# Inside each product of the feed-forward pairs: rounded weights first, the remainder's passes behind them

## Chip, core and metric

One core of a Trainium2 chip runs the whole kernel. The metric is the device time of one execution in microseconds (us); the time of a kernel is the median of several runs. Five engines matter here: TensorE (PE, with its weight loads shown apart as PEld), VectorE (DVE), ScalarE (ACT), GpSimd (POOL, which here mostly issues DMAs that add one tile to another) and SyncE (SP, which issues the loads).

## The reference, cut to what matters

The block is a state-space and short-convolution mixer followed by a gated feed-forward part; 512 positions, model width 2048, feed-forward width 5632. The change is in the first product of the feed-forward part, `xn @ w_up`:

```python
def conv_ffn(xn, w_up, ffn_conv_w, ffn_conv_b, w_down):
    h = xn @ w_up                                       # (512, 2048) @ (2048, 11264)
    a = causal_dwconv(h[..., :D_FF], ffn_conv_w, ffn_conv_b)
    return (jax.nn.gelu(a) * h[..., D_FF:]) @ w_down
```

Everything is float32. The result must be that of float32 products.

## The kernel before

**Three passes for one product.** TensorE is fed with the type fp32r. A weight tile W is split on the chip into a rounded part hi (ACT, line 152, tile `whi`) and the remainder lo = W - hi (DVE, line 131, tile `wlo`), and the activations likewise into xh and xl. A 128x128 block of a product is then three passes of TensorE that add into the same PSUM tile: hi on xh, hi on xl, lo on xh. Each pass is one weight load (PEld) and one matmul (PE); the hi block is loaded twice, once for xh and once for xl.

**Chunks.** All weight tiles of the kernel stand in one list, `flat`; an entry is 128 partitions by up to 1024 elements, that is up to 8 blocks (j = 0 to 7). `whi` and `wlo` have three buffers each. The passes of an entry are emitted first, and then, in `after` or `after_pair`, what ACT and DVE do for the entries that follow: `prep_to(i + 3)` emits the rounding and the remainder of the entry two places on. The order on each engine is the order in which the Python code emits it; nothing reorders it later.

**The feed-forward pairs.** For each of 44 blocks of feed-forward channels both halves of `w_up` are needed, each over 2048 inputs: four weight tiles of 1024 by 128. The first block is done plainly (units `ua` and `ub`, 512 columns of moving data per pass, `products` outside the class). The other 43 are the class `Pair` (G = 1 to 43): sums and differences of the four tiles are multiplied with sums and differences of the activations of the two sequence halves (LO and HI, 256 columns each), so that seven products replace eight. A pair has seven entries, here called products c = 0 to 6, each of 8 blocks and so of 24 passes over 256 columns. Lines 1041, 1042 and 1043 are the three passes: hi on xh, hi on xl, lo on xh. Moving data are `x2h`/`x2l`, `th`/`tl` and, for c = 6, the tile `xga`. The PSUM tiles are called `sr`.

**What runs around a product.** After product c, `after_pair` emits `sums(c)` (reads of finished PSUM tiles: ACT lines 1050 and 1059, DVE lines 1053 to 1063), the rounding for the entry two places on, the remainders that are due (`lo_all`), and `rest(c)`: sums of raw weights for the next pair (DVE lines 995 and 1007, ACT copy line 1001, and POOL's adding DMAs, lines 996 and 1008), loads of the pair after that (SP, line 984), and the steps of the gate of the previous pair (convolution on DVE, lines 1072 and 1075, and the gelu on ACT, line 1076). So, in a steady pair, ACT has the gelu of the previous pair (emitted after product 1) ahead of the rounding for product 4 (emitted after product 2), and that gelu waits for a convolution step on DVE.

**Where the other order is already in use.** `products` for all other units (lines 164 to 173) first runs through hi on xh and hi on xl for all blocks and then through lo on xh. Those have 512 columns, but for the last eight units of the kernel (`ends`), which have 256.

Of the kernel before, what the change touches and what calls it, by code (L numbers as in the profile page):

```python
# [16 lines left out]
P = 128  # L17
# [50 lines left out]
def block_kernel(ctx: ExitStack, tc: tile.TileContext, a: dict):  # L68
    nc = tc.nc
# [88 lines left out]
    def products(i, j0, j1):  # L158

        u, c = flat[i]  # L160
        if u.ps is None:
            u.ps = psm.tile([P, T], F32, tag="mm", name="mm")
        base = sum(x[1] for x in u.chunks[:c])
        hi, lo = preps[i]
        for j in range(j0, j1):
            xh, xl = (x[:, u.cols] for x in u.xs(base + j))
            w = slice(j * P, (j + 1) * P)
            nc.tensor.matmul(u.ps[:, u.cols], hi[:, w], xh, start=base + j == 0, stop=False)  # L168
            nc.tensor.matmul(u.ps[:, u.cols], hi[:, w], xl, start=False, stop=False)  # L169
        for j in range(j0, j1):  # L170
            xh = u.xs(base + j)[0][:, u.cols]
            nc.tensor.matmul(u.ps[:, u.cols], lo[:, j * P:(j + 1) * P], xh, start=False,  # L172
                             stop=base + j == u.total - 1)
# [35 lines left out]
    def run(i0, i1):  # L209
        for i in range(i0, i1):  # L210
            u, c = flat[i]
            if u.chunks[c][0] is None:
                u.products(i, c)
                after_pair(i)
                continue
            if c == 0 and u.pre:
                u.pre()
            products(i, 0, u.chunks[c][1])
            after(i)
# [454 lines left out]
    for i in range(3, 19):  # L674
        u, c = flat[i]
        u.hooks.setdefault(c, []).append(lambda: next(params))

    def start():
# [40 lines left out]
        for z in zpad:  # L719
            nc.vector.memset(z[:, 0:2], 0.0)  # L720
        products(0, 0, 6)
        products(1, 0, 6)
        products(0, 6, 8)
        preps.pop(0)
# [285 lines left out]
    class Pair:  # L1010
# [21 lines left out]
        def products(self, i, c):  # L1032
            hi, lo = preps[i]
            name = ("p1", "px", "p6", "py", "p1", "px", "py")[c]
            if c < 4:
                self.ps[name] = ff["pss"].tile([P, T], F32, tag="sr", name="sr")[:, 0:T // 2]
            ps = self.ps[name]
            for j in range(8):
                xh, xl = self.moving(c, j)
                w = slice(j * P, (j + 1) * P)  # L1040
                nc.tensor.matmul(ps, hi[:, w], xh, start=(c < 4 and j == 0), stop=False, skip_group_check=c >= 4)  # L1041
                nc.tensor.matmul(ps, hi[:, w], xl, start=False, stop=False, skip_group_check=c >= 4)  # L1042
                nc.tensor.matmul(ps, lo[:, w], xh, start=False, stop=j == 7, skip_group_check=c >= 4)  # L1043


        def sums(self, c):
# [250 lines left out]
```

## Time and profile before

| | |
|---|---|
| median of 3 runs | 2515.23 us (2514.97 to 2516.53) |
| the profiled execution | 2517.59 us, its span 2515.6 us |
| granted TensorE clock, mean | 0.997 |
| busy: PE / PEld / DVE / ACT / POOL | 2482.3 / 2184.4 / 1665.4 / 1079.2 / 565.4 us |
| pairs on PE: first matmul to start of the last | 1166.5 to 2017.5 us of the span |

A PE that is "busy" in a profile is not a PE at its peak: a matmul is shown from its start to its modelled end (0.28 us here), while the next one starts 0.11 to 0.12 us after it. What passes cost is therefore read from the distance between starts, and waits from the idle time before weight loads.

### The profile page before, as it was taken

How to read it: one execution, taken by the hardware profiler on the slowest of the kernel's cores; microseconds unless marked ns; L12 is line 12 of the kernel's file. 1: busy time of each engine (PE TensorE's matmuls, PEld its weight loads, DVE VectorE, ACT ScalarE, POOL GpSimd, SP SyncE). 2: the span in 40 equal slices, each digit the busy share in tenths (PEclk: the TensorE clock that was granted, in tenths of full speed). 3: DMA queues.
4: the chain of work that ended last, by engine and by line, in shares of the span. 5: the costliest groups of instructions: out<-in, count | busy, mean ns of one | idle time of the engine just before them, and what ended most of it. 6: DMA issues, size and time to landing. Idle time of an engine off the chain costs nothing.

```text
span 2515.6 us, 36421 instructions
## 1 busy us (share of the span) xinstructions
PE 2482.3 (99%) x14616; PEld 2184.4 (87%) x14616; DVE 1665.4 (66%) x1924; ACT 1079.2 (43%) x1384; POOL 565.4 (22%) x424
## 2 busy tenths in 40 slices
PE   8999999999999999999999999999999999999997
PEld 6888888777888888888999999999999988888887
DVE  7799889999224464447777777887777753333334
ACT  5355444553234333335455544555454432222233
POOL 1077777778003121110000000000000000000011
PEclk9999999999999999999999999999999999999998
DMA  5777777786345344444666666666666663434335
GB/s 180 228 191 189 186 189 202 192 208 185 132 167 184 109 142 139 151 138 144 174 174 167 170 184 180 184 177 176 182 181 175 197 243 115 129 112 128 97 93 160
DMA packets 149209, 418.40 MB, mean 166 GB/s; under 512 B 17712, under 2 KB 26032, under 8 KB 149040
## 3 DMA queue, kind: packets, MB, share of 16 engines
q1 hardware_dynamic: 121584, 330.88, 41.4%
q0 software_dynamic: 20448, 74.46, 15.8%
q10 hardware_dynamic: 7008, 10.74, 1.2%
q8 instruction: 114, 1.87, 0.3%
q14 instruction: 55, 0.45, 0.1%
HBM read 300.67 MB, written 40.89 MB: 136 GB/s over the span
## 4 chain that ended last, share of the span: by engine, by line
PE 84%; DVE 7%; DMA 4%; issue 3%; ACT 2%; SPq 0%; DVEq 0%; ACTq 0%; POOLq 0%
PE mm L168 19%; PE mm L169 19%; PE mm L172 19%; PE sr L1043 8%; PE sr L1042 8%; PE sr L1041 8%; DVE wlo L131 2%; DMA wraw<-wraw 2%; ACT whi L152 2%; DVE zz L487 1%; DVE wraw L995 1%; DVE ph L452 0%; PE w L476 0%; DMA braw<-in_b 0%; DMA xgb<-xgb 0%
## 5 line engine op out<-in xcount | busy, mean ns | idle before, releaser
L131 DVE TENSOR_TENSOR wlo<-wraw,whi 128x1024 fp32r<-128x1024 f32 (+1 forms) x396 | 486.0, 1228 | 325.7 <-ACT whi L152 287.1
L152 ACT ACTIVATE whi<-wraw 128x1024 fp32r<-128x1024 f32 (+1 forms) x396 | 393.9, 998 | 382.3 <-PE mm L169 332.6
L168 PE MATMUL mm<-xh,whi 128*128 128x512 f32 x1344 | 527.6, 393 | 10.6 <-ACT whi L103 5.8
L169 PE MATMUL mm<-xl,whi 128*128 128x512 f32 x1344 | 526.0, 391 | 0.0
L1043 PE MATMUL sr<-x2h,wlo 128*128 128x256 f32 x1376 | 386.5, 281 | 2.9 <-DVE wlo L131 1.6
L1041 PE MATMUL sr<-x2h,whi 128*128 128x256 f32 x1376 | 383.4, 279 | 0.8 <-ACT whi L152 0.8
L1042 PE MATMUL sr<-x2l,whi 128*128 128x256 f32 x1376 | 383.3, 279 | 0.0
L172 PE MATMUL mm<-xh,wlo 128*128 128x512 f32 x1344 | 332.9, 389 | 2.4 <-DMA wlo<-wraw 2.4
L168 PEld LDWEIGHTS mm<-xh,whi 128*128 128x128 f32 x1344 | 253.5, 189 | 72.2 <-ACT whi L103 5.8
L172 PEld LDWEIGHTS mm<-xh,wlo 128*128 128x128 f32 x1344 | 252.1, 188 | 56.4 <-DMA wlo<-wraw 4.1
L169 PEld LDWEIGHTS mm<-xl,whi 128*128 128x128 f32 x1344 | 253.5, 189 | 54.3 <-DVE xl L108 1.8
L1043 PEld LDWEIGHTS sr<-x2h,wlo 128*128 128x128 f32 x1376 | 258.9, 188 | 6.9 <-DVE wlo L131 6.5
L1041 PEld LDWEIGHTS sr<-x2h,whi 128*128 128x128 f32 x1376 | 259.0, 188 | 1.1 <-ACT whi L152 1.0
L1042 PEld LDWEIGHTS sr<-x2l,whi 128*128 128x128 f32 x1376 | 259.7, 189 | 0.0
L1043 PE MATMUL sr<-th,wlo 128*128 128x256 f32 x688 | 192.2, 279 | 1.3 <-DVE wlo L131 1.3
L1042 PE MATMUL sr<-tl,whi 128*128 128x256 f32 x688 | 192.0, 279 | 0.0
L168 PE MATMUL mm<-x2h,whi 128*128 128x512 f32 (+1 forms) x528 | 191.9, 371 | 0.0
L1041 PE MATMUL sr<-th,whi 128*128 128x256 f32 x688 | 191.9, 279 | 0.0
L169 PE MATMUL mm<-x2l,whi 128*128 128x512 f32 (+1 forms) x528 | 191.2, 369 | 0.0
L875 POOL TENSOR_TENSOR acc<-acc,sq 128x512 f32<-128x512 f32 (+1 forms) x31 | 38.8, 1250 | 641.9 <-ACT sq L873 641.9
L131 DVE TENSOR_TENSOR wlo<-r,whi 128x1024 fp32r<-128x1024 f32 x88 | 107.5, 1222 | 49.2 <-ACT whi L152 49.2
L1008 POOL DMA_DIRECT2D wraw<-wraw x43 | 37.0, 861 | 446.8 <-DVE ap L1061 422.2
(253 smaller groups left out, 4593.2 us busy)
## 6 DMA issues: line engine op xcount, KB each, us to landing
wraw<-in_w_in SPq DMA_DIRECT2D x127, 512.0 KB, 4.3
r<-in_w_up SPq DMA_DIRECT2D x88, 512.0 KB, 5.9
xgb<-in_w_up SPq DMA_DIRECT2D x84, 512.0 KB, 5.3
wraw<-in_w_down SPq DMA_DIRECT2D x104, 384.0 KB, 3.2
wlo<-wraw POOLq DMA_DIRECT2D x56, 512.0 KB, 5.4
wraw<-wraw POOLq DMA_DIRECT2D x43, 512.0 KB, 9.6
wraw<-in_w_o SPq DMA_DIRECT2D x32, 512.0 KB, 3.6
r<-r POOLq DMA_DIRECT2D x22, 512.0 KB, 4.6
```

Source lines behind the costliest of these rows:

```text
L131: nc.vector.tensor_tensor(o, x, y, op=ALU.subtract)
L152: nc.scalar.activation(hi[:, w], raw[:, w], AF.Copy)
L168: nc.tensor.matmul(u.ps[:, u.cols], hi[:, w], xh, start=base + j == 0, stop=False)
L169: nc.tensor.matmul(u.ps[:, u.cols], hi[:, w], xl, start=False, stop=False)
L172: nc.tensor.matmul(u.ps[:, u.cols], lo[:, j * P:(j + 1) * P], xh, start=False, stop=base + j == u.total - 1)
L487: nc.vector.tensor_tensor(z, z, t, op=ALU.subtract if j else ALU.add)
L875: nc.gpsimd.tensor_tensor(acc[:, cols], acc[:, cols], ff["sq"][:, cols], op=ALU.add)
L995: nc.vector.tensor_tensor(s, r[:, 2], r[:, 3], op=ALU.add)
L1008: nc.gpsimd.dma_start(gs[G]["s4"], s, accum_op=ALU.add)
L1041: nc.tensor.matmul(ps, hi[:, w], xh, start=(c < 4 and j == 0), stop=False, skip_group_check=c >= 4)
L1042: nc.tensor.matmul(ps, hi[:, w], xl, start=False, stop=False, skip_group_check=c >= 4)
L1043: nc.tensor.matmul(ps, lo[:, w], xh, start=False, stop=j == 7, skip_group_check=c >= 4)
```

## The change

Within one product of a pair the order of the 24 passes changes. Before, each block j had its three passes together. Now the 16 passes with hi (two for each block) come first and the 8 with lo behind them. Nothing else is touched: the passes, their operands, the PSUM tile and what all other engines are given stay as they are.

```diff
                 w = slice(j * P, (j + 1) * P)
                 nc.tensor.matmul(ps, hi[:, w], xh, start=(c < 4 and j == 0), stop=False, skip_group_check=c >= 4)
                 nc.tensor.matmul(ps, hi[:, w], xl, start=False, stop=False, skip_group_check=c >= 4)
-                nc.tensor.matmul(ps, lo[:, w], xh, start=False, stop=j == 7, skip_group_check=c >= 4)
+            for j in range(8):
+                nc.tensor.matmul(ps, lo[:, j * P:(j + 1) * P], self.moving(c, j)[0], start=False, stop=j == 7,
+                                 skip_group_check=c >= 4)
```

On PE, at the beginning of the first product of pair 1, the program before has these rows (line, operation, output<-moving,weights; in brackets the semaphores waited for: those of ACT for the rounded weights, those of DVE for the remainder):

```order
L1041 MATMUL sr<-x2h,whi 128x256 [waits Activation_49]
L1042 MATMUL sr<-x2l,whi 128x256
L1043 MATMUL sr<-x2h,wlo 128x256 [waits DVE_49]
L1041 MATMUL sr<-x2h,whi 128x256
L1042 MATMUL sr<-x2l,whi 128x256
L1043 MATMUL sr<-x2h,wlo 128x256
```

The end of the same product in the changed program, and the start of the next one (a row with x7 stands for seven alike):

```order
L1041 MATMUL sr<-x2h,whi 128x256
L1042 MATMUL sr<-x2l,whi 128x256
L1041 MATMUL sr<-x2h,whi 128x256
L1042 MATMUL sr<-x2l,whi 128x256
L1044 MATMUL sr<-x2h,wlo 128x256 [waits DVE_49]
L1044 MATMUL sr<-x2h,wlo 128x256 x7
L1041 MATMUL sr<-th,whi 128x256 [waits Activation_49]
```

The wait for the remainder has moved from the third pass of a product to its seventeenth; the wait for the rounded weights stays on the first. Line 1043 of before is line 1044 in the changed kernel.

On ACT, in pair 2 of the program before, these rows run from the rounding for product 3 to the copy of product 4's PSUM tile:

```order
L152 ACTIVATE whi<-r 128x1024 [waits DMASW4_49,Activation_49]
L1076 ACTIVATE cv<-cv 128x512 [waits DVE_49]
L152 ACTIVATE whi<-r 128x1024 [waits PE_49,Activation_49]
L152 ACTIVATE whi<-wraw 128x1024 [waits DMASW5_49,PE_49,Activation_49]
L1001 ACTIVATE wraw<-xgb 128x1024 [waits DMAHW2_49]
L1059 ACTIVATE ap<-sr 128x256 [waits PE_49]
```

In the changed program the same place reads:

```order
L152 ACTIVATE whi<-r 128x1024 [waits DMASW4_49,Activation_49]
L1078 ACTIVATE cv<-cv 128x512 [waits DVE_49]
L152 ACTIVATE whi<-r 128x1024 [waits PE_49,Activation_49]
L152 ACTIVATE whi<-wraw 128x1024 [waits DMASW5_49,PE_49,Activation_49]
L1001 ACTIVATE wraw<-xgb 128x1024 [waits DMAHW2_49]
L1061 ACTIVATE ap<-sr 128x256 [waits PE_49]
```

Only line numbers differ (1076 is 1078, 1059 is 1061): ACT, and DVE likewise, keep their order. The second row is the gelu, the third the rounding for product 4, behind it.

## Rows read from the trace of the kernel before

**Rows 1.** The page, part 1: busy us (share of span) xinstructions.

```profile
PE 2482.3 (99%) x14616; PEld 2184.4 (87%) x14616; DVE 1665.4 (66%) x1924; ACT 1079.2 (43%) x1384; POOL 565.4 (22%) x424
```

**Rows 2.** Lines 1043 and 1041: ns min/median/max, first and last start, forms.

```profile
L1043 PE MATMUL sr<-xga,wlo x344: 276/281/388, 1185.5 to 2017.5; 128*128 128x256 f32 x172
...
L1041 PE MATMUL sr<-x2h,whi x1376: 276/280/387, 1166.5 to 2014.5; 128*128 128x256 f32 x197
```

**Rows 3.** Who waited for whom: us in total, times, longest us.

```profile
PEld sr L1043 <- DVE wlo L131: 9.7, 25, 1.5
```

**Rows 4.** PE timeline (start us, us), pair 4: first and last of 105 consecutive matmuls.

```profile
1229.73 0.28 PE L1042 MATMUL sr<-xga,whi 128*128 128x256 f32 x1
...
1241.97 0.28 PE L1041 MATMUL sr<-x2h,whi 128*128 128x256 f32 x1
```

**Rows 5.** PE timeline, pairs 26 and 27: first and last of 108 consecutive matmuls.

```profile
1681.78 0.28 PE L1042 MATMUL sr<-xga,whi 128*128 128x256 f32 x1
...
1693.92 0.28 PE L1041 MATMUL sr<-x2h,whi 128*128 128x256 f32 x1
```

**Rows 6.** Groups on PE, 1167:1172, 1230:1242, 1682:1694 us: busy us, mean ns.

```profile
L1041 PE MATMUL sr<-th,whi 128*128 128x256 f32 x8 | 2.2, 281 | 0.0
...
L1041 PE MATMUL sr<-x2h,whi 128*128 128x256 f32 x17 | 4.8, 281 | 0.0
...
L1043 PE MATMUL sr<-th,wlo 128*128 128x256 f32 x16 | 4.4, 276 | 0.0
```

**Rows 7.** Stretches: us, then PE, PEld, DVE, ACT, POOL busy (x), PEclk, DMA share, GB/s.

```profile
1700.00:1900.00 200.00, 199.38 (x1707) 198.00 (x1706) 158.26 (x195) 101.43 (x123) 18.06 (x21) 1.00 0.66 176
...
2100.00:2300.00 200.00, 200.00 (x884) 165.62 (x883) 71.65 (x91) 50.05 (x66) 0.00 (x0) 1.00 0.41 119
```

**Rows 8.** PEld timeline: 6 of the 26 weight loads that waited, idle and releaser bracketed.

```profile
1173.84 0.19 PEld L1043 LDWEIGHTS sr<-th,wlo 128*128 128x128 f32 x1 [1.47 <-DVE wlo L131]
...
1197.69 0.19 PEld L1041 LDWEIGHTS sr<-x2h,whi 128*128 128x128 f32 x1 [1.03 <-ACT whi L152]
...
1202.49 0.19 PEld L1043 LDWEIGHTS sr<-x2h,wlo 128*128 128x128 f32 x1 [0.73 <-DVE wlo L131]
...
1655.48 0.19 PEld L1043 LDWEIGHTS sr<-x2h,wlo 128*128 128x128 f32 x1 [0.29 <-DVE wlo L131]
...
1681.09 0.19 PEld L1043 LDWEIGHTS sr<-xga,wlo 128*128 128x128 f32 x1 [0.28 <-DVE wlo L131]
...
1931.27 0.19 PEld L1043 LDWEIGHTS sr<-x2h,wlo 128*128 128x128 f32 x1 [0.28 <-DVE wlo L131]
```

**Rows 9.** Timelines of ACT, then DVE, before product 4 of pair 25.

```profile
1652.59 0.63 ACT L1076 ACTIVATE cv<-cv 128x512 f32<-128x512 f32 x1 [3.27 <-DVE cv L1075]
1653.12 1.05 ACT L152 ACTIVATE whi<-r 128x1024 fp32r<-128x1024 f32 x1
...
1651.81 0.74 DVE L1075 SCALAR_TENSOR_TENSOR cv<-ap,vec,cv 128x512 f32<-128x512 f32 x1
...
1654.20 1.23 DVE L131 TENSOR_TENSOR wlo<-r,whi 128x1024 fp32r<-128x1024 f32 x1 [0.84 <-ACT whi L152]
```

**Rows 10.** PE timeline: the lo pass that waited there, and the next pass.

```profile
1655.48 0.39 PE L1043 MATMUL sr<-x2h,wlo 128*128 128x256 f32 x1
1655.71 0.28 PE L1041 MATMUL sr<-x2h,whi 128*128 128x256 f32 x1
```

**Rows 11.** Timelines of DVE, POOL and ACT in pairs 1 and 2.

```profile
1175.91 1.22 DVE L131 TENSOR_TENSOR wlo<-r,whi 128x1024 fp32r<-128x1024 f32 x1
...
1186.98 0.85 POOL L996 DMA_DIRECT2D xgb<-xgb  x1 [19.80 <-DVE ap L1061]
...
1196.58 1.06 ACT L152 ACTIVATE whi<-xgb 128x1024 fp32r<-128x1024 f32 x1 [4.34 <-DMA xgb<-xgb]
```

**Rows 12.** Groups on PE in the last units, 2465 to 2480, then 2488 to 2500 us.

```profile
L172 PE MATMUL mm<-x2h,wlo 128*128 128x256 f32 x43 | 6.4, 281 | 0.0
...
L172 PE MATMUL mm<-x2h,wlo 128*128 128x256 f32 x31 | 4.5, 276 | 0.0
```

## Prediction

> **What bounds the kernel now.** I read the page first. The reader is to see that TensorE is busy for 2482.3 us of the span and no other engine for more than 1665.4 [rows 1], so a change on another engine's path counts only where PE waits for it. In the pairs PE runs from 1166.5 to 2017.5 us, and with the last pass that is 851.1 us [rows 2] for 43 x 7 x 24 = 7224 passes.
>
> Second, the waits of these lines. In the chain of waits the loads of lo weights stood 9.7 us in 25 places until DVE had the remainder [rows 3]; the timeline of the loads has one more, 1.03 us for hi weights until ACT had rounded [rows 8]. That is 10.7 us, 0.4% of the kernel. Each also costs a refill: after such a wait the next pass comes 0.23 us behind the one that waited [rows 10], twice the usual distance, so some 0.115 us more. Waits and refills are 10.7 + 26 x 0.115 = 13.7 us.
>
> Third, the distance between starts, which the page doesn't show. Pair 4 goes from 1229.73 to 1241.97 in 104 steps: 117.7 ns a pass [rows 4]. Pairs 26 and 27 go from 1681.78 to 1693.92 in 107 steps: 113.5 ns [rows 5]. There are no large waits within either. So there are **two paces**. They show in the duration of one matmul as well: 281 ns in the first of these stretches and 276 in the second [rows 6], and 276 and about 281 are minimum and median over all pairs [rows 2]. The granted clock is 1.00, the level of 2.4 GHz, around the quick stretch as elsewhere [rows 7]. In the 512-column units 884 passes take 200 us [rows 7], 226.2 ns or 113.1 for each 256 columns; the quick pace is that of streaming, and the slow one has 4.2 ns on top. Without waits the pairs take (851.1 - 13.7)/7224 = 115.9 ns a pass, so (115.9 - 113.5)/4.2, some 57%, run at the slow pace.
>
> What sets the pace? I followed the timeline from wait to wait. In undisturbed passes the pace stays as it is, over several products and pairs. It changes where a lo load comes late: the slow stretch of pair 4 lies behind the wait at 1202.49, the quick one behind that at 1681.09 [rows 8]. Taking the duration of the passes behind each of the 25 lo waits (the first at 1173.84, the last at 1931.27 [rows 8]), I find 276 ns after 16 and 281 after 9. A wait is a throw of a coin, and the side it shows holds until the next. That is my reading of a pattern; the trace doesn't name the cause.
>
> **The change, part by part.** No pass is added or removed, so the work of PE, loads included, is unchanged. The last 256-column units already run in the new order, and they show both paces, 281 ns and then 276 [rows 12]: the order as such fixes neither, and I take nothing for it.
>
> *The lo waits.* The lo weights are needed 14 passes later, at 113.5 to 117.7 ns each 1.59 to 1.65 us. The typical wait, at product 4 of a pair, is 0.29 us [rows 8]. Its chain: the gelu of the previous pair holds ACT until 1653.12, the rounding ends at 1654.17, the remainder at 1655.43 [rows 9]. The product had begun at about 1655.0 (the lo load at 1655.48 less its idle 0.29 and the 0.19 of the load before it). In the new order lo is wanted at about 1655.0 + 16 x 0.1135 - 0.1 = 1656.7, 1.3 us after it is there. What is late next there is hi, and it is not: it was there 0.8 us before the product. ACT and DVE keep their order; a hi buffer comes free 7 passes earlier, which can only help. So I cost all waits from pair 3 on at nothing. The cover is DVE's spare time: 158.26 us busy in 200 [rows 7], about 15.7 per pair, against 168 x 0.1135 = 19.1.
>
> *The start of the stretch* is another matter, since DVE and ACT are behind there and some waits return. At 1173.84 lo had been waited for 1.47 us, inside the 1.65 of a slow start: gone, just. Product 3 of pair 1 then begins 1.6 us earlier, but its remainder still ends at 1175.91 + 1.22 = 1177.13 [rows 11] and is wanted at about 1176.8: 0.3 us. In pair 2 the hi of product 3 waits for a tile to which POOL's DMA adds, issued at 1186.98; it is rounded by 1196.58 + 1.06 = 1197.64 [rows 11]. With PE 1.7 us ahead that issue moves up by about as much (it hangs on a PSUM tile of pair 1 through ACT and DVE): hi at about 1196.0, PE there at about 1194.9, so 1.1 us instead of 1.03. Behind it stand the remainder, a convolution step, the gelu and the next rounding (1.23 + 0.74 + 0.63 + 1.05 = 3.65 us by the durations in [rows 9]) against 2.8 us of product 3, so product 4 waits 0.8 us for hi, where it had waited 0.73 for lo. Together 2.2 us, with three refills 2.5; bounds are 0 (the DMA lands early) and 5 (all waits up to 1202.49 come back).
>
> *The pace* decides the rest. After the last of these waits, near 1199, nothing throws the coin again for about 6960 passes. The quick side came up 16 times in 25.
>
> The sum for the quick side: 88 passes at the entry at 117.7 = 10.4; 176 between the first and the last wait at the mean 115.9 = 20.4; 6960 x 0.1135 = 790.0; waits 2.5: 823.3 us, **27.8 less** than 851.1. From the profiled execution's 2517.59 (2.0 us more than its span, which I leave as they are) that gives 2489.8; the median of the runs lies 2.4 below that execution, so 2487.4. All behind the pairs moves up unchanged.
>
> [...]
>
> **The rivals.**
> *Locked slow.* The last throw falls on the other side: 7048 x 0.1177 + 20.4 + 2.5 = 852.4, that is 1.3 us more than now, 2516.5: no change that can be told. For it speaks that PE enters the pairs at the slow pace, 281 ns a matmul in their first 5 us [rows 6], and that 9 of 25 throws went so.
> *Only the waits go.* The pace keeps a mixture, because lateness too small for the list of waits still throws the coin, or because a pace is not held as I think: 7224 x 0.1159 + 2.5 = 839.8, 11.3 less, 2503.9. For it speaks that the cause of the paces is not named by any view; against it, that the changes which I could place stood at late lo loads, and these now have over 1 us. [...]
> *Hi late in every pair.* Slower than before: with the lo waits gone, PE reaches product 4 earlier against ACT's chain through the gelu, and the wait comes back on hi, x us in each of 42 pairs. At the mixed pace that is 839.8 + 42 (x + 0.115); it passes 856.1 (0.2% above now) at x = 0.27. Hi has 0.8 us of slack, so the chain would have to slip by 1.1. For x = 0.6 it would be 869.8, the kernel 2533.9. Against it: that chain starts at the end of product 0 of the same pair and moves with PE.
>
> **How the numbers follow.** Quick 50% (16 in 25, less what the other cases take), locked slow 26%, mixed 18%, hi late 6%. The forecast is the quick case, 2487.4, for itself 2483 to 2493 (start waits from 0 to 5 us, a pace of 113.1 to 113.8). To hold 8 in 10 the range must reach through the mixed case to the slow one: 2483 to 2518. A measurement of this kernel tells about 0.2%, 5.0 us, from no change. Faster: quick and nearly all mixed, 67%; within 0.2%: locked slow and the rest of mixed, 27%; slower: 6%.
>
> **What would show it.** In the changed profile the loads of line 1044 should have almost no idle time, and those of line 1041 about 2 us, all before 1205. The mean duration of the passes of pairs 3 to 43 should be 276 ns and 1762 of them fit in 200 us (1699 if locked slow, 281 ns). The forecast is wrong if passes change between 276 and 281 where no load waits, if new waits stand at hi in the steady pairs, or if the coin falls on the slow side; the waits alone are worth less than half of it.

## The result, and the profile after

The changed kernel took **2487.24 us** (median of 18 runs), the kernel before 2515.05 us beside it: ratio 0.9914, 95% interval 0.9897 to 0.9932. Its runs are spread as those of before are not: 2483.11 to 2519.72 us, against 2511.82 to 2518.00. In a second series of 12 runs (the experiment e7_after_again) the median was 2496.19 us, ratio 0.9945 (0.9914 to 0.9976). Of all 30 runs 17 lie below 2493 us, 9 between 2495 and 2512, and 4 above 2515. So the gain is real, some 0.5 to 0.9% in the median, but one run may have all of it or nothing. One run of a kernel below, e8_hi_late, took 3088.64 us at a mean granted clock of 0.752, where its six others have 0.996 or 0.997, and its ratio leaves that run out.

The profiled execution, 2485.59 us, is one of the quick ones. Its rows answer to those of before in the same order. First the page's busy times, to be held against [rows 1]:

```profile
PE 2457.0 (99%) x14616; PEld 2163.2 (87%) x14616; DVE 1656.0 (67%) x1924; ACT 1075.1 (43%) x1384; POOL 569.8 (23%) x424
```

PE lost 25.3 us of busy time with the same 14616 matmuls. That number alone would say that matmuls got cheaper; which ones is read from the lines of the pairs (ns min/median/max, first and last start), against [rows 2]:

```profile
L1044 PE MATMUL sr<-xga,wlo x344: 276/276/277, 1181.6 to 1984.6; 128*128 128x256 f32 x172
...
L1041 PE MATMUL sr<-x2h,whi x1376: 276/276/388, 1162.7 to 1980.8; 128*128 128x256 f32 x197
```

The median duration fell from about 281 to 276 ns, and the pairs now run from 1162.7 to 1984.6 us, 822.0 us with the last pass, instead of 851.1. Stretches of 200 us in them (PE, PEld, DVE, ACT and POOL busy with counts, PEclk, DMA share, GB/s), against the 1707 passes of [rows 7]:

```profile
1300.00:1500.00 200.00, 200.00 (x1767) 200.00 (x1766) 160.84 (x199) 103.07 (x127) 18.06 (x21) 1.00 0.69 182
1500.00:1700.00 200.00, 200.00 (x1768) 200.00 (x1767) 166.97 (x208) 107.44 (x134) 17.20 (x20) 1.00 0.69 187
1700.00:1900.00 200.00, 200.00 (x1765) 199.87 (x1764) 161.47 (x201) 102.91 (x127) 18.94 (x22) 1.00 0.68 184
```

Such a count takes in the matmuls that reach over the edges of its window, some two of them, so a pace that is worked out from it is 0.1 ns too low. From start to start, two passes that are 4000 passes apart:

```profile
1279.07 0.28 PE L1044 MATMUL sr<-xga,wlo 128*128 128x256 f32 x1
...
1732.40 0.28 PE L1041 MATMUL sr<-x2h,whi 128*128 128x256 f32 x1
```

That is 113.3 ns a pass: the quick pace, at the same granted clock. The chain of waits (it leaves out what is shorter than 0.15 us), in the stretch of the pairs, has two rows for these loads, against one of 9.7 us in [rows 3]:

```profile
PEld sr L1041 <- ACT whi L152: 2.0, 2, 1.3
...
PEld sr L1044 <- DVE wlo L131: 0.3, 1, 0.3
```

and the timeline of the loads shows where the three are (idle and releaser in brackets), against [rows 8]:

```profile
1173.35 0.98 PEld L1044 LDWEIGHTS sr<-x2h,wlo 128*128 128x128 f32 x8 [0.31 <-DVE wlo L131]
...
1191.99 0.19 PEld L1041 LDWEIGHTS sr<-x2h,whi 128*128 128x128 f32 x1 [1.34 <-ACT whi L152]
...
1195.52 0.19 PEld L1041 LDWEIGHTS sr<-x2h,whi 128*128 128x128 f32 x1 [0.64 <-ACT whi L152]
```

All three stand in pairs 1 and 2. Behind the last of them the passes take 276 ns to the end of the pairs; one more load was late there, by 0.13 us, too little for the list (hi at product 4 of pair 31, below).

### The profile page after: what moved, and what is told of

The parts are those of the page before. It is cut to its first block, busy times and chain, and to the rows that moved or that the text cites. A ratio compares the mean times of both kernels' runs of the same rounds, so it can differ in the third digit from the quotient of the medians.

```text
span 2483.5 us, 36421 instructions
## 1 busy us (share of the span) xinstructions
PE 2457.0 (99%) x14616; PEld 2163.2 (87%) x14616; DVE 1656.0 (67%) x1924; ACT 1075.1 (43%) x1384; POOL 569.8 (23%) x424
## 4 chain that ended last, share of the span: by engine, by line
PE 88%; DVE 7%; DMA 2%; issue 2%; ACT 1%; POOL 0%; SPq 0%; DVEq 0%; ACTq 0%; POOLq 0%
PE mm L168 19%; PE mm L169 18%; PE mm L172 18%; PE sr L1044 11%; PE sr L1041 11%; PE sr L1042 11%; DVE zz L487 1%; DVE wlo L131 1%; DVE ph L452 1%; DVE ph L462 1%; DVE dt L100 1%; DVE zz L100 1%; DVE bst L448 0%; DMA wraw<-wraw 0%; DVE zz L488 0%
## 5 line engine op out<-in xcount | busy, mean ns | idle before, releaser
L1041 PE MATMUL sr<-x2h,whi 128*128 128x256 f32 x1376 | 320.9, 276 | 1.6 <-ACT whi L152 1.6
L1042 PE MATMUL sr<-x2l,whi 128*128 128x256 f32 x1376 | 320.6, 276 | 0.0
L1044 PE MATMUL sr<-x2h,wlo 128*128 128x256 f32 x1376 | 184.1, 276 | 0.1
L1044 PEld LDWEIGHTS sr<-x2h,wlo 128*128 128x128 f32 x1376 | 168.8, 188 | 0.3 <-DVE wlo L131 0.3
L1041 PE MATMUL sr<-th,whi 128*128 128x256 f32 x688 | 160.3, 276 | 0.0
L1042 PE MATMUL sr<-tl,whi 128*128 128x256 f32 x688 | 160.3, 276 | 0.0
L488 DVE TENSOR_TENSOR_SCAN zz<-sm_mag,zz 128x512 f32<-128x512 f32 x64 | 136.7, 2136 | 2.2
```

Source lines behind the costliest of these rows:

```text
L488: nc.vector.tensor_tensor_scan(z, mag[:, p:p + 1].to_broadcast([P, T]), z, 0.0, op0=ALU.mult, op1=ALU.add)
L1044: nc.tensor.matmul(ps, lo[:, j * P:(j + 1) * P], self.moving(c, j)[0], start=False, stop=j == 7, skip_group_check=c >= 4)
```

## The experiments

Eight kernels ran in two series; in each the kernel before ran beside them (medians 2510.22 and 2514.23 us), and the ratios are to that. The question is what made the passes quicker: that no late load throws the pace any more (theory W), the grouping by weights (O), only the waits themselves (R), or a pace that drifts (D).

W needs a word on what "late" means. A weight load that had to wait starts 0.05 us after the end of the rounding or the remainder that it waited for. By this mark loads can be found that were late by less than the list of waits shows. In the trace of the kernel before the pace changes 34 times: 11 times at waits of that list, 23 times at lo loads that were late by less, the least by some 7 ns. One of these, in pair 9, shows the remainder of product 2 and its first lo load, and hi passes ahead of it (1322.5 to 1334 us) and behind it (1335.2 to 1340 us):

```profile
1333.27 1.23 DVE L131 TENSOR_TENSOR wlo<-wraw,whi 128x1024 fp32r<-128x1024 f32 x1 [1.62 <-ACT whi L152]
```

```profile
1334.55 0.19 PEld L1043 LDWEIGHTS sr<-th,wlo 128*128 128x128 f32 x1
```

```profile
L1041 PE MATMUL sr<-x2h,whi 128*128 128x256 f32 x19 | 5.2, 276 | 0.0
...
L1041 PE MATMUL sr<-x2h,whi 128*128 128x256 f32 x8 | 2.2, 281 | 0.0
```

**e1_lag4: less grouping, and no late loads either.** Lo stands four blocks behind hi: 8 hi passes come first, then hi and lo mixed (two hi, one lo, four times over), and the last 4 lo passes together. The diff is cut to the loop and the lo pass:

```diff
-            for j in range(8):
+            for s_ in range(8 + 4):
...
+                if s_ >= 4:
+                    j = s_ - 4
+                    nc.tensor.matmul(ps, lo[:, j * P:(j + 1) * P], self.moving(c, j)[0], start=False, stop=j == 7,
```

> Interleaved again, but each block's lo pass stands four blocks behind its hi passes: lo is first wanted on the 11th pass (before: 3rd; changed kernel: 17th), 0.9 us later than before, so the steady waits of 0.29 us should be gone while hi and lo passes still alternate. Theory W (a late load throws the pace, and without late loads it holds; the order itself is nothing): as the changed kernel, most runs near 2487 us, idle time of the lo loads under 2 us, all of it in pairs 1 and 2, passes of the steady pairs at 276 ns. Rival O (grouping the passes by weights is what makes them quick): only the waits go, passes of both 276 and 281 ns, near 2504 us.

Measured: 2487.72 us median of 12 runs, 2485.23 to 2519.19, ratio 0.9942 (0.9912 to 0.9972). Seven runs are below 2490, two at 2496 to 2498, three above 2516. O asked for 2504; this order, with half of its lo passes among the hi passes, has quick runs like those of the grouped one. As the other half still stand together, this alone does not rule out O; e2 and e4 do. The profiled run (2496.34 us) is one of those between, and shows how they come about. Two stretches, then DVE's and the load's rows at the place where the pace changes, in pair 28:

```profile
1300.00:1500.00 200.00, 200.00 (x1767) 200.00 (x1766) 160.86 (x199) 103.08 (x127) 18.05 (x21) 1.00 0.69 183
...
1700.00:1900.00 200.00, 200.00 (x1700) 200.00 (x1700) 157.59 (x195) 99.63 (x121) 18.08 (x21) 1.00 0.65 177
```

```profile
1685.94 1.23 DVE L995 TENSOR_TENSOR wraw<-r 128x1024 f32<-128x1024 f32 x1 [0.62 <-DMA r<-in_w_up]
```

```profile
1696.45 0.19 PEld L1043 LDWEIGHTS sr<-xga,whi 128*128 128x128 f32 x1 [0.15 <-ACT whi L152]
```

First 1767 passes in 200 us, later 1700. Between them DVE stood 0.62 us until a load from memory had landed, ACT's rounding fell behind, and hi came late at products 4 (by 0.06 us, too little for the list of waits) and 6. The pace turned slow at the first of these, quick again at the lo load of product 4, which was late too, and slow for good at the lo load of product 6, behind this remainder:

```profile
1696.43 1.23 DVE L131 TENSOR_TENSOR wlo<-xgb,whi 128x1024 fp32r<-128x1024 f32 x1 [0.53 <-ACT whi L152]
```

```profile
1697.71 0.19 PEld L1047 LDWEIGHTS sr<-xga,wlo 128*128 128x128 f32 x1
```

That load stood for 0.05 us, and is not in the list of waits either. After it the slow pace, 281 ns, held to the end of the pairs with no late load at all.

**e2_lo_first: grouped, but with the late loads back.** The 8 lo passes stand ahead of the 16 hi passes:

```diff
+            for j in range(8):
+                nc.tensor.matmul(ps, lo[:, j * P:(j + 1) * P], self.moving(c, j)[0], start=(c < 4 and j == 0),
+                                 stop=False, skip_group_check=c >= 4)
             for j in range(8):
...
-            for j in range(8):
-                nc.tensor.matmul(ps, lo[:, j * P:(j + 1) * P], self.moving(c, j)[0], start=False, stop=j == 7,
-                                 skip_group_check=c >= 4)
```

> Grouped as in the changed kernel, but the 8 lo passes come first and the 16 hi passes behind them: lo is wanted on the first pass, 0.23 us earlier than in the kernel before, so the waits come back longer, about 0.6 us at product 4 and 0.25 at products 2 or 6 of every pair. W: the pace is thrown in every pair and passes of 276 and 281 ns alternate in stretches, at least a quarter of them at 281; with 41 x 1.1 us of waits and refills about 2545 us. O: waits as large, but 276 ns throughout, about 2534 us.

Measured: 2530.63 us (4 runs), ratio 1.0079 (1.0066 to 1.0092). The wait row of the pairs, and the durations of hi passes in two stretches (busy us, mean ns), 1300 to 1327 and 1390 to 1400 us:

```profile
PEld sr L1039 <- DVE wlo L131: 23.1, 91, 2.0
```

```profile
L1044 PE MATMUL sr<-x2h,whi 128*128 128x256 f32 x55 | 12.8, 276 | 0.0
...
L1044 PE MATMUL sr<-th,whi 128*128 128x256 f32 x16 | 3.9, 281 | 0.0
```

Both paces are back in a grouped order, 31% of the passes at 281 ns by my count of the timeline. That is W and not O. The time lies nearer to O's number than to W's, because I put the waits at 41 x 1.1 us and they were 23.1 with 91 refills, 33.6 in all.

**e4_lag1: lo one block behind.** As e1, with 1 in the place of 4, so that but for the first and the last passes of a product two hi passes and one lo pass alternate throughout.

> Each block's lo pass stands one block behind: lo is first wanted on the 5th pass, 0.23 us later than before, so the wait at product 4 should shrink from 0.29 to some 0.06 us in quick pairs, and to nothing in slow ones. W: lateness that small still throws the pace, passes of both 276 and 281 ns, 2495 to 2512 us. If only long waits throw it: 276 ns throughout, near 2487. O: also a mixture, 2504, but then the lag of 4 gives the same.

Measured: 2512.79 us (12 runs, 2506.22 to 2519.70), ratio 1.0008 (0.9996 to 1.0020): no gain, and just above W's 2495 to 2512, though only six lo loads are left in the list of waits, 3.6 us, and one hi load, 2.2 us. The profiled run (2516.99 us) holds both paces. Hi passes from 1430 to 1570 us, the last wait, and the stretch behind it:

```profile
L1043 PE MATMUL sr<-x2h,whi 128*128 128x256 f32 x225 | 60.8, 276 | 0.0
```

```profile
1579.39 0.19 PEld L1047 LDWEIGHTS sr<-xga,wlo 128*128 128x128 f32 x1 [0.29 <-DVE wlo L131]
```

```profile
1580.00:1980.00 400.00, 400.00 (x3399) 400.00 (x3398) 318.66 (x394) 203.11 (x248) 35.28 (x41) 1.00 0.67 179
```

From 1401 to 1579 us the passes are quick although lo is some 0.05 us late at product 4 of each pair; a wait of 0.29 us at 1579.39 turns them slow, and they stay slow for 22 pairs in which no load is late, 3399 in 400 us (117.8 ns from start to start). So the slow pace holds by itself as well, and an alternating order can be quick, against O. Lateness of 0.05 us did not throw the pace here in nine pairs; but in pair 2 of the same trace, at 1190.25 us, a lo pass that was as late (0.153 us behind the one before it, in place of 0.113) turned the quick pace slow. Lateness that small can throw the pace, as W had it, and need not.

**e5_before_gelu_late: the old order with the wait at product 4 taken away.** The gelu moves behind the rounding for product 4 on ACT:

```diff
                 nc.vector.scalar_tensor_tensor(self.cv, z[:, 0:T], V("fw", n), self.cv, op0=ALU.mult, op1=ALU.add)
-                nc.scalar.activation(self.cv, self.cv, AF.Gelu_apprx_tanh)
             elif step == 3:
+                nc.scalar.activation(self.cv, self.cv, AF.Gelu_apprx_tanh)
```

> The order of before, with only the wait at product 4 taken away: the gelu of the previous pair stands behind the rounding for product 4 on ACT. The lo loads of product 4 should not wait from pair 3 on; those of products 2 and 6 still come within some 0.01 us of the moment at which they are wanted in quick stretches, and 0.3 us late in pairs 20 to 28. W: with most throws gone a slow stretch, in which no load is late, holds for many pairs, while quick stretches still get thrown, so more passes are slow than before; the saved waits are given back: 2500 to 2517 us, with 281 ns over most of the steady pairs. Rival R (waits cost only themselves): 8 to 11 us less than before, with the mixture of before.

Measured: 2518.40 us (11 runs, 2515.20 to 2520.21), ratio 1.0013 (1.0004 to 1.0021), 1.4 us above W's 2500 to 2517. Waits and two stretches:

```profile
PEld sr L1043 <- DVE wlo L131: 2.2, 3, 1.4
```

```profile
1500.00:1700.00 200.00, 200.00 (x1700) 200.00 (x1699) 161.53 (x201) 106.14 (x128) 17.63 (x21) 1.00 0.68 185
1700.00:1900.00 200.00, 200.00 (x1701) 200.00 (x1700) 156.29 (x193) 101.85 (x123) 17.26 (x20) 1.00 0.66 176
```

The lo waits fell from 9.7 us to 2.2, and the kernel got no faster. The passes behind the last of these waits are slow, 7028 of them, and behind the last late load of all, 0.15 us in pair 2, there are 6980. This decides against R: 7.5 us of waits were saved and given back by the pace. The waits I expected in pairs 20 to 28 did not come, since at the slow pace lo is in time.

**e8_hi_late: hi late in every pair.** In the changed kernel two copies of the gelu's tile onto itself delay ACT:

```diff
                 nc.scalar.activation(self.cv, self.cv, AF.Gelu_apprx_tanh)
+                for _ in range(2):
+                    nc.scalar.activation(self.cv, self.cv, AF.Copy)
```

> The changed kernel with two copies of the gelu's tile onto itself (0.63 us each) behind the gelu on ACT, so that the rounding for product 4 is some 1.1 us later and hi, not lo, is late there by 0.3 to 0.4 us in every steady pair. W: each such wait throws the pace, passes of 276 and 281 ns in stretches, with 41 x (0.35 + 0.115) us of waits and refills 2510 to 2520. If only a late lo load throws it: 276 ns throughout, about 2506.

Measured: 2522.69 us (7 runs), ratio 1.0028 (1.0017 to 1.0039). The wait row, two neighbouring waits, and hi passes behind the one and the other:

```profile
PEld sr L1041 <- ACT whi L152: 25.9, 47, 2.0
```

```profile
1258.25 0.19 PEld L1041 LDWEIGHTS sr<-x2h,whi 128*128 128x128 f32 x1 [0.59 <-ACT whi L152]
...
1278.38 0.19 PEld L1041 LDWEIGHTS sr<-x2h,whi 128*128 128x128 f32 x1 [0.28 <-ACT whi L152]
```

```profile
L1041 PE MATMUL sr<-x2h,whi 128*128 128x256 f32 x26 | 6.3, 281 | 0.0
...
L1041 PE MATMUL sr<-x2h,whi 128*128 128x256 f32 x24 | 5.6, 276 | 0.0
```

Here one pair is slow and the next quick; in the whole trace the pace changes 26 times, each time at a late load, 23 times at one in the list of waits. A late hi load throws the pace as a late lo load does, and this is the rival "hi late in every pair" made real: 0.28% more than before in spite of the new order. The time is above W's 2510 to 2520; I had put in waits of 0.35 us, and most were 0.59. A small part is the clock: behind a wait of 1.97 us in pair 2 the granted clock was 0.51, the level of 1.2 GHz, from 1198.2 to 1201.6 us, and 16 passes stood 0.213 us apart, 1.6 us more than at the quick pace; e2 has such a stretch as well.

**e6_after_gelu_late, e7_after_again, e9_gelu_late_again: where the runs between come from.** e7 is the changed kernel once more; e6 and e9 are the same kernel, the change with the gelu moved as in e5.

> The changed kernel with the gelu of the previous pair emitted one product later on ACT, behind the rounding for product 4 instead of ahead of it, so that hi of product 4 is there some 1.5 us earlier. W: no load of hi weights waits from pair 3 on and the wait of 0.6 us at product 4 of pair 2 goes; the runs between 2490 and 2515 us become rare (in the changed kernel 6 of 18), the median is 2483 to 2488. Rival D (the pace drifts by itself, without a late load): such runs are as many as before, a third of them.

> The changed kernel once more, for its spread beside the kernel that follows. W: most runs between 2483 and 2489, about a third between 2490 and 2520; if the profiled one is among these, its change to 281 ns stands at a load that waited. D (drift): at a place where none did.

> The changed kernel with the gelu behind the rounding for product 4, again, for more of its runs. W: no hi load waits from pair 3 on, so none of its runs changes pace under way; all runs are near 2485, or, when the one long wait in pair 2 falls on the slow side, near 2516, and none is between 2490 and 2510. D: a third of them lies between.

Measured: e6 2485.40 us (4 runs, 2482.87 to 2487.01), ratio 0.9899 (0.9886 to 0.9911); e9 2485.19 us (4 runs, 2482.53 to 2492.24), ratio 0.9888 (0.9873 to 0.9903); e7, beside e9, 2496.19 us (12 runs, 2484.46 to 2520.85). All eight runs with the late gelu are below 2493, of the changed kernel's 17 in 30; drawing eight of all 38 runs would give that by chance about once in 45 times. Two expectations were missed: one run of e9 took 2492.24 us, where none was to lie between 2490 and 2510, and in e7 only 5 of 12 runs, not most, lie between 2483 and 2489. The rows at pair 31 of e7 show what goes wrong: DVE's sum of raw weights, ACT's rounding for product 4, and the load of hi on PE:

```profile
1744.09 1.22 DVE L995 TENSOR_TENSOR wraw<-xgb 128x1024 f32<-128x1024 f32 x1 [1.93 <-DMA xgb<-in_w_up]
```

```profile
1747.68 1.04 ACT L152 ACTIVATE whi<-r 128x1024 fp32r<-128x1024 f32 x1
```

```profile
1748.78 0.19 PEld L1041 LDWEIGHTS sr<-x2h,whi 128*128 128x128 f32 x1 [1.28 <-ACT whi L152]
```

DVE stood 1.93 us until a load from memory had landed, and the remainder, the convolution step, the gelu and the rounding behind it all slipped; hi of product 4 was 1.28 us late. The pace was thrown there and fell on the quick side, so this run was quick, 2486.18 us. The profiled run of the changed kernel has a milder case at the same place. The rows are DVE's, then the rounding for product 4 and the load of hi in pair 30, where nothing is late, then both in pair 31:

```profile
1743.22 1.23 DVE L995 TENSOR_TENSOR wraw<-xgb 128x1024 f32<-128x1024 f32 x1 [0.77 <-DMA xgb<-in_w_up]
```

```profile
1726.91 1.04 ACT L152 ACTIVATE whi<-xgb 128x1024 fp32r<-128x1024 f32 x1
...
1728.66 0.19 PEld L1041 LDWEIGHTS sr<-x2h,whi 128*128 128x128 f32 x1
```

```profile
1746.81 1.04 ACT L152 ACTIVATE whi<-r 128x1024 fp32r<-128x1024 f32 x1
...
1747.91 0.19 PEld L1041 LDWEIGHTS sr<-x2h,whi 128*128 128x128 f32 x1
```

In pair 30 hi was there 0.71 us before its load, 0.05 of which a load needs: a slack of some 0.65 us, the same in the other steady pairs. DVE's wait of 0.77 us used it up and left hi 0.13 us late; in e7 1.93 us left it 1.28 us late. In e9 DVE waits for memory at the same place, for nearly as long as in the changed kernel, but no load on PE waits behind it:

```profile
1740.58 1.23 DVE L995 TENSOR_TENSOR wraw<-xgb 128x1024 f32<-128x1024 f32 x1 [0.72 <-DMA xgb<-in_w_up]
```

```profile
PEld sr L1041 <- ACT whi L152: 1.5, 1, 1.5
```

In pair 30 of e9 the rounding for product 4 is the second of these two, done at 1721.45 us, and its load comes 4.62 us later:

```profile
1719.45 2.00 ACT L152 ACTIVATE whi<-xgb 128x1024 fp32r<-128x1024 f32 x2
```

```profile
1726.08 0.19 PEld L1041 LDWEIGHTS sr<-x2h,whi 128*128 128x128 f32 x1
```

So moving the gelu gave hi 3.9 us more slack, where I had expected 1.5. The only hi wait of e9 is the one in pair 2. D is not borne out: the pace changes 111 times in the ten traces, always at a late load (65 times at one in the list of waits), and never where no load was late. That the unprofiled runs of 2495 to 2512 us are all of this kind is argued from e1's profile and from their absence in e6 and e9, not shown run by run.

## Why the prediction was right, and where it was off

**The forecast** was 2487.4 us, by the quick case; measured were 2487.24 and, in the second series, 2496.19. The first agreement to 0.2 us is partly luck of the draw. It is luck in another way too: the two profiled executions differ by 32.0 us, of which 29.1 lie in the pairs (27.8 were forecast) and 3.8 ahead of them, where both kernels are the same; behind the pairs 0.8 went back. The step that carried it, that removing late loads lets a pace hold and so is worth more than the waits, is shown from both sides: e1, with late loads gone and less grouping, is as quick, and e5, with most waits gone and the old order, is not.

**The order as such costs nothing**: right. e1 and the changed kernel have the same quick time, and the grouped e2 has both paces.

**The lo waits** go: right. One of 0.31 us is left, where 0.3 was forecast, and none in the steady pairs.

**The start**: 0.3, 1.1 and 0.8 us were forecast, 0.31, 1.34 and 0.64 came, together 2.29 against 2.2. The first pass of the pairs is slow, as forecast, and the pairs took 822.0 us against 823.3 in the sum. The pace of 113.5 ns was a little high; it is 113.3 from start to start. That of 512 columns is 226.7 by the same measure, not 226.2.

**"Nothing throws the coin again for about 6960 passes"**: this step was too strong. I gave hi 0.8 us of slack (it has 0.65) and put the cover at DVE's spare time, but did not count that a load from memory that lands late takes this slack away. In the profiled run one did, and hi was about 0.1 us late in pair 31; in e7 it was 1.28 us late; in e1 it turned the pace. By their times 9 of 30 runs are mixed, where I gave 18%, 4 are locked slow, where I gave 26%, and 17 are quick, where I gave 50%; 30 runs are too few to say that these chances were wrong.

**That "the side it shows holds until the next"**, said of the 25 lo waits in the list, was wrong. Between them the pace changed 23 times in the trace of the kernel before, at lo loads late by less than 0.15 us. So the cause that I named for the mixed case, lateness too small for the list of waits, is at work: in e1 the last change of pace stands at a lo load that was 0.05 us late, behind a hi load that had waited 0.15. Where that lateness came from is what I had not seen: a load from memory.

**The coin** is not a fair one, and its odds depend on the side that lies up. Behind late loads in e8 a quick pace stayed quick 24 times in 37 and a slow one became quick 13 times in 14 (waits of the list, and on the slow side three shorter ones). What an order makes of it depends on which pace has no late loads. Before, both had some: 0.29 us at product 4 and some 0.01 us at products 2 and 6 in the quick pace, some 0.05 us at product 4 in the slow, so it switched all the time. In e5 only the quick pace had any left, as I read it (the trace is slow from pair 2 on), and by their times the slow one kept all 11 runs. With the change neither has, and each run keeps what the last wait of pair 2, or a late load, leaves it. This reading fits all eight kernels; why a pass takes 4.4 ns more at one pace, and what decides which pace a late load leaves, is not settled by any of them.

**Hi late in every pair** did not happen in the changed kernel, as 6% had said; e8 shows that it would have cost what was gained and more.

## What to carry to other kernels

Where a busy engine runs a stream of short passes, measure the distance between starts in several stretches before costing a wait: here 4% of pace hung on waits that made up 0.4% of the time, and on lateness too short for the list of waits. Order work so that the operand that is ready last is read last, and then look at the next operand in line and give it slack too: the gelu moved behind the rounding made the gain hold in all eight of its runs. And when the runs of a kernel spread more than before, profile several of them; a median of a few runs can fall on either side.

## What the runs showed of the hardware

TensorE has two paces for passes with 256 moving columns and a weight load each, at a granted clock of 1.00 in both: 113.3 ns from start to start (matmul records of 276 ns) and 117.8 ns (281 ns). Either holds without any late load over thousands of passes, 6981 quick ones in e9 and 6980 slow ones in e5, and each of the 111 changes in ten traces stands at a weight load that had waited, some for 7 ns. Such a load starts 0.05 us after the end of the operation that it waited for. Coming from passes of 512 columns the pairs began slow in all nine traces taken after the prediction, as they had before. With 512 columns one pace was seen, 226.7 ns (2100 to 2300 us of the kernel before).
